# mLSTM steps put ahead of attention's in the emission order, and side work on TensorE emitted only where its operands are modelled as ready some time ahead

## The chip, the cores and the metric

The kernel runs on one core of one Trainium2 chip. A core has TensorE (PE) for matmuls, VectorE (DVE), ScalarE (ACT) and GpSimd (POOL) for elementwise work, and SyncE (SP), whose queue issues the transfers. Each engine takes its own instructions in order; semaphores hold an instruction back until what it reads has been written. The metric is the device time of one execution in microseconds, as the median of several runs. Before the change it was 1105.98 us over three runs (1102.45 to 1107.39).

## The reference

One layer of a decoder, for a prompt of 512 positions and a group of 8 samples of one position each, which share all weights (D_MODEL 1024, all in float32):

```python
z = rmsnorm(h) @ w_in                       # q, k, v of attention; q, k, v, o, gates of the mLSTM; two gates
o_a = attention of three dilation groups, 12 heads of 64, merged by softmax of their log sums
      # prompt: banded blocks of 128;  sample: 129 gathered positions of the caches per head
qk = silu(causal_conv(z[..., OFF_MQ:OFF_MV], conv_buf, conv_w, conv_b))
hm, C1, n1, m1 = mlstm(qm, km, vm, ig, lf, C0, n0, m0)   # 4 heads of 256, chunked scan over the prompt,
                                                         # one step for each sample with its state C0
o_b = rmsnorm_per_head(hm) * mh_norm * sigmoid(z_o)
mix = sigmoid(g_a) * (o_a @ w_proj_a) + sigmoid(g_b) * (o_b @ w_proj_b)
h = h + mix @ w_out
h = h + (silu(xf @ w_gate) * (xf @ w_up)) @ w_down       # xf = rmsnorm(h)
h = h + sigmoid(xp @ w_ple_gate) * (p @ w_ple_proj)      # xp = rmsnorm(h)
```

It returns the normed outputs, the updated key and value caches, the convolution rows, and the mLSTM states C, n and m of the prompt and of the samples.

## The kernel before

**Dense work.** The weights stream through in chunks of 512 rows. Each is split in two float32r parts, whi (a cast on ScalarE or VectorE) and wlo (the rest, on VectorE), and so is the activation (xnh and xnl, or "pieces"). A product is three matmuls, hi by hi, hi by lo and lo by hi, on halves of 260 columns (512 + 8 positions make 520). The products with w_pb and with the gate and up weights of the feed-forward part go by seven combined products instead of eight, which need sums of weights (ws) and sums of activations (ta, tb, piece). The order of all dense jobs is one list, `order`; `dense_to` (line 672) walks through it.

**Side work.** Everything else is written as Python generators that `yield` a condition and then emit an instruction: attention of the prompt (`attn_prompt`), of the samples (`attn_sample`), the mLSTM of the prompt (`mlstm_prompt`) and of the samples (`sample_rows`, `sample_loads`, `mlstm_sample` with its two `steps`, `sample_sums`), the evictions and norms. Between the matmuls of a dense product `dense_to` calls `feed`, which loads and splits weights ahead, and `pr.run()` of the class `Procs` (line 305), which goes through all waiting generators, evictions (`evs`) first, then `live` in the order in which they were spawned, and lets each go on as far as its condition holds.

**What sets the order.** While it emits, the program keeps a model of the five engines, `Clock`: for each a time at which it is free, and for each tile the time at which it is written and read. The condition `on(engs, *tiles, **rooms)` (line 271) asks whether the rings of the named tags have room and whether the tiles are ready in the model: for TensorE at the model's present time, for others within a limit. If no dense product can go on, `stall` moves the model's TensorE 0.1 on. The settings in `PAR` are by stage: A to the end of the products with w_in that attention and the mLSTM need (variable `n_win`), then B, C and D.

**Rings.** Tiles come from rings by tag. S has five slots: attention's loaded cache rows (kvb, in triples, one for each dilation group), the state tiles ct of the mLSTM and others share it. P1 and P2 hold the broadcast rows qb and kb of the samples' mLSTM, and later the tanh tiles of the gates (th), which are to be written only when the last `sample_loads` is done. PSUM has two pairs of banks for dense results (pp) and four banks b for the rest.

**Names in the rows.** All instructions are issued through one helper, so each row carries its line, L225. pT is the transposed softmax of sample attention, `pT,kvb` its product with loaded value rows; qkm the samples' q and k rows; yc the convolved rows, whose last step also leaves nout; numv and dns the numerators and denominators of the samples' mLSTM; W0 to W3 the prompt's mLSTM weights; scs the scores of sample attention; raw a loaded weight.

Of the kernel before, what the change touches and what calls it, by code (L numbers as in the profile page):

```python
# [32 lines left out]
def kernel(tc, a):  # L33
# [8 lines left out]


PAR = {
    "A": dict(LIM=1.8, SLACK=1.5, THIN=0.8, BIAS=0.3, EVLIM=2.0, PLIM=0.3),
    "B": dict(LIM=0.8, SLACK=0.51, THIN=0.8, BIAS=0.24, EVLIM=1.97, PLIM=0.01),
    "C": dict(LIM=1.59, SLACK=0.52, THIN=0.8, BIAS=0.02, EVLIM=2.16, PLIM=0.5),
    "D": dict(LIM=1.28, SLACK=1.14, THIN=0.8, BIAS=0.32, EVLIM=1.71, PLIM=0.38),
}


# [178 lines left out]
def _body(nc, a, const, sb, psp, drp):  # L230
# [10 lines left out]
    def tl(tag, name, shape=None, dt=F32):  # L241
        w = WIDTH.get(tag, 520)
        if tag in used:
            used[tag] += 1
        return ck.new(sb.tile(list(shape or (128, w)), dt, name=name, tag=tag, bufs=NB[tag]), tag, NB[tag])
# [8 lines left out]
    def bank(shape=(128, 512)):  # L254
        used["b1"] += 1
        return ck.new(psp.tile(list(shape), F32, name="b1", tag="b1", bufs=4), "b1", 4)
# [7 lines left out]
    def free(n, tag):  # L264
        used[tag] -= n
# [3 lines left out]
    P = dict(PAR["A"])  # L269

    def on(engs, *tiles, lim=None, **rooms):

        engs = engs.split()

        def ok():
            for tag, n in rooms.items():
                if tag in used and used[tag] + n > NB[tag]:
                    return False
            now = ck.t["pe"]
            for tag, n in rooms.items():  # L280
                i = ck.count.get(tag, 0)
                if any(ck.idle(tag, i + j, NB[tag]) > now + P["SLACK"] for j in range(n)):
                    return False
            if engs[0] == "pe":
                t = now
            else:
                t = min(ck.t[e] for e in engs)
                if t > now + (P["LIM"] if lim is None else lim):
                    return False
                t = max(t, now) + 0.1  # L290
            return all(ck.ready(x) <= t for x in tiles)
        return ok

    class Cycle:
        def __init__(self, tags):
            self.tags, self.i = tags, 0

        def next(self, n):
            return [self.tags[(self.i + k) % len(self.tags)] for k in range(n)]
# [4 lines left out]

    class Procs:
        def __init__(self):
            self.evs, self.live = [], []

        def spawn(self, gen, first=False):
            (self.evs if first else self.live).append([None, gen])  # L310

        def run(self):
            for q in (self.evs, self.live):
                for p in list(q):
                    while p[0] is None or p[0]():
                        try:
                            p[0] = next(p[1])
                        except StopIteration:
                            q.remove(p)
                            break  # L320

    pr = Procs()
# [35 lines left out]
    def copy(dst, src, names=("act", "dve")):  # L358
        n = pick(names, "tensor_copy", dst, [src])
        if n == "act":  # L360
            S_.copy(dst, src)
        else:
            ENG[n].tensor_copy(dst, src)
# [5 lines left out]
    def stt(dst, x, sc, y, op0, op1):  # L369
        V.scalar_tensor_tensor(dst, x, sc, y, op0=op0, op1=op1)  # L370
# [956 lines left out]
    def sample_rows(h):  # L1327

        yield lambda: all(("k", h, dt) in ml for dt in range(2)) and "rows" in flag
        yield on("pe", qkm, b1=1, S=1)  # L1330
        bk = bank((8, 2, 2, 128))
        rows = tl("S", "mrows", (8, 2, 256))
        for w in range(2):
            for dt in range(2):
                PE.transpose(bk[:, w, dt], qkm[:, h, w, dt], ident)
        yield on("act dve", bk)
        copy(rows.rearrange("b w d -> b (w d)"), bk.rearrange("b w t d -> b (w t d)"))
        free(1, "b1")
        yield on("sp", rows)
        dr = drp.tile([8, 2, 256], F32, name="mdr", tag="mdr", bufs=2)  # L1340
        SP.dma_start(dr.rearrange("b w d -> b (w d)"), rows.rearrange("b w d -> b (w d)"))
        free(1, "S")
        mdr[h] = dr
# [18 lines left out]
    def mlstm_sample(h):  # L1362
        yield lambda: (h, 0) in cts and all(("v", h, vt) in ml for vt in range(2))
        yield on("dve", vm, s24b)
        vw = sb.tile([128, 2, 8], F32, name="vw", tag="vw", bufs=2)
        V.tensor_tensor(vw, vm[:, h], s24b[:, h, 8:16].unsqueeze(1).to_broadcast([128, 2, 8]), op=ALU.mult)
        numv = sb.tile([128, 2, 8], F32, name="numv", tag="numv", bufs=2)
        left = [8]

        def steps(b0):  # L1370
            for b in range(b0, 8, 2):
                yield lambda: (h, b) in cts
                cur = cts.pop((h, b))
                qb, kb = qks[h, b - b % 2]
                yield on("act dve", cur, s24b)
                if pick(("act", "dve"), "tensor_scalar", cur, [cur]) == "act":
                    S_.activation(cur, cur, AF.Copy, scale=s24b[:, h, b:b + 1])
                else:
                    V.tensor_scalar(cur, cur, s24b[:, h, b:b + 1], None, op0=ALU.mult)
                for vt in range(2):  # L1380
                    yield on("dve", cur, kb, vw)
                    stt(cur[:, vt], kb[:, b % 2], vw[:, vt, b:b + 1], cur[:, vt], ALU.mult, ALU.add)
                for vt in range(2):
                    yield on("dve", cur, qb)
                    V.tensor_tensor_reduce(junk, cur[:, vt], qb[:, b % 2], 1.0, 0.0, ALU.mult, ALU.add,
                                           numv[:, vt, b:b + 1])
                left[0] -= 1
                done[b] = True
                if b ^ 1 in done:
                    free(1, "P1")  # L1390
                    free(1, "P2")
                store(a["C_s"][h, b], cur, lambda: free(1, "S"))

        done = {}
        for b0 in range(2):
            pr.spawn(steps(b0))
        yield lambda: left[0] == 0
        pr.spawn(sample_sums(h, numv))

    def sample_sums(h, numv):  # L1400

        nn = nout[:, h, :, 1:9]
        w_i = s24b[:, h, 8:16].unsqueeze(1).to_broadcast([128, 2, 8])
        w_x = s24b[:, h, 0:8].unsqueeze(1).to_broadcast([128, 2, 8])
        nt = small(32, "nt").rearrange("p (t c) -> p t c", t=2)
        tv = nt[:, :, 0:8]
        V.tensor_tensor(tv, qkm[:, h, 1], w_i, op=ALU.mult)
        V.tensor_tensor(nn, nst[:, h], w_x, op=ALU.mult)
        V.tensor_tensor(nn, nn, tv, op=ALU.add)
        V.tensor_tensor(tv, nn, qkm[:, h, 0], op=ALU.mult)  # L1410
        V.tensor_tensor(nt[:, :, 8:16], numv, numv, op=ALU.mult)
        yield on("pe", nt, b1=1)
        bk = bank((128, 16))
        for t in range(2):
            PE.matmul(bk, ones, nt[:, t], start=t == 0, stop=t == 1)

        dn = sb.tile([128, 16], F32, name="dns", tag="dns", bufs=2)
        yield on("act", bk)
        S_.activation(dn[:, 0:8], bk[:, 0:8], AF.Abs)
        V.tensor_copy(dn[:, 8:16], bk[:, 8:16])  # L1420
        free(1, "b1")
        yield on("dve", dn)
        V.tensor_tensor(dn[:, 0:8], dn[:, 0:8], s24b[:, h, 16:24], op=ALU.max)
        ml["ns", h] = True
        yield lambda: ("og", h, 0) in ml and ("og", h, 1) in ml
        yield from sample_out(h, numv, dn)
# [163 lines left out]
    def chain(*gens):  # L1590
        for g in gens:
            yield from g
# [113 lines left out]
    def loads():  # L1706
        for c in "0a123":
            if c == "a":
                yield lambda: "vs" in flag
            else:  # L1710
                yield from sample_loads(int(c))
# [4 lines left out]
    for c in "apm":  # L1716
        if c == "a":
            pr.spawn(chain(attn_prompt(0), attn_prompt(1)))
        elif c == "p":
            pr.spawn(chain(*[mlstm_prompt(h) for h in range(4)]))  # L1720
        else:
            pr.spawn(samples())
            pr.spawn(loads())
            pr.spawn(chain(*[sample_rows(h) for h in range(4)]))
            pr.spawn(chain(*[mlstm_sample(h) for h in range(4)]))

    oa = []

# [393 lines left out]
    for h in range(2):  # L2122
        pr.spawn(last_norm(h))
    dense_to(len(order))
    while pr.evs or pr.live:
        stall()
    while copies:
        cache_copy()
# [141 lines left out]
```

## Time and profile before

| | us |
|---|---|
| median of 3 runs (lowest to highest) | 1105.98 (1102.45 to 1107.39) |
| profiled execution | 1104.25 |
| its span in the trace | 1102.5 |
| TensorE busy | 1050.2 (95%) |
| VectorE busy | 859.1 (78%) |
| ScalarE busy | 522.8 (47%) |
| GpSimd busy | 35.8 (3%) |
| mean granted clock of TensorE | 0.979 of full |

The span is the time between the first and the last instruction in the trace; the rest of the profiled execution, 1.75 us, lies around it. Idle time of an engine is shown with what ended it. The granted clock is the share of full speed that TensorE was given: 1.00 is 2.4 GHz and 0.50 is 1.2 GHz. A time in the text is counted from the start of the span. "Dense columns" count the columns of the dense matmuls emitted so far; they give a place in the program that is the same in both kernels, since the list of dense jobs isn't changed.

### The profile page before, as it was taken

Reading aid. Unit: us, or ns where it says so; the run is one execution under the profiler, and the core shown is the slowest. Engines: PE = TensorE matmul, PEld = TensorE weight load, DVE = VectorE, ACT = ScalarE, POOL = GpSimd, SP = SyncE. Lnnn points to the kernel's source line nnn. Section 1 sums busy time; section 2 is a strip of 40 time slices with the busy share of each in tenths; the row PEclk is TensorE's granted clock in tenths of the full one; section 3 lists DMA queues with packets and bytes.
Section 4 is the critical chain, followed back from the end, with each engine's and each line's share of the span. In section 5 each row is a group of like instructions: output and inputs, shape, how many; then the busy total and the mean of one; then the engine's idle time right before and its main releaser. Section 6 shows DMA issues by size and latency. Waiting matters only on the chain.

```text
span 1102.5 us, 21771 instructions
## 1 busy us (share of the span) xinstructions
PE 1050.2 (95%) x8404; PEld 1026.4 (93%) x8404; DVE 859.1 (78%) x1768; ACT 522.8 (47%) x968; POOL 35.8 (3%) x126
## 2 busy tenths in 40 slices
PE   7999999999998999997999999989999999999995
PEld 6999899999998989996999999989999999999995
DVE  7994559877778599876466868999888888866775
ACT  6445444664454487754343335435344434433553
POOL 0010010001001011000000000000000000000000
PEclk9999999999997999998999999999999999999998
DMA  6365157747846986876566833322323332333321
GB/s 229 118 201 174 58 193 244 269 150 227 269 138 218 309 268 197 268 213 227 197 210 233 283 103 96 121 84 92 103 83 108 111 101 83 110 94 97 120 83 59
DMA packets 90904, 180.21 MB, mean 163 GB/s; under 512 B 11604, under 2 KB 37252, under 8 KB 89392
## 3 DMA queue, kind: packets, MB, share of 16 engines
q1 hardware_dynamic: 90800, 178.82, 50.5%
q8 instruction: 66, 1.08, 0.4%
q14 instruction: 38, 0.31, 0.1%
HBM read 163.65 MB, written 59.13 MB: 202 GB/s over the span
## 4 chain that ended last, share of the span: by engine, by line
PE 67%; DVE 15%; DMA 8%; ACT 5%; issue 3%; SPq 1%; POOL 0%; DVEq 0%; ACTq 0%
PE pp L225 42%; PE b L225 25%; DVE wlo L225 3%; DMA raw<-in_w_in 3%; DVE yc L225 2%; ACT whi L225 2%; DMA out_C_s<-ct 1%; DMA ct<-in_sC 1%; DMA qb<-mdr 1%; DVE ct L225 1%; SPq L225 1%; DVE junk L225 1%; DVE piece L225 1%; DVE sw L225 1%; DVE h L225 1%
## 5 line engine op out<-in xcount | busy, mean ns | idle before, releaser
L225 DVE TENSOR_TENSOR wlo<-raw,whi 128x512 fp32r<-128x512 f32 (+3 forms) x358 | 236.6, 664 | 148.1 <-ACT whi L225 134.5
L225 ACT CAST whi<-raw 128x512 fp32r<-128x512 f32 (+3 forms) x340 | 203.1, 601 | 290.8 <-PE pp L225 155.3
L225 PE MATMUL b<-piece,whi 128*128 128x260 f32 x1232 | 229.3, 287 | 10.0 <-ACT piece L225 6.0
L225 PE MATMUL pp<-xnh,whi 128*128 128x260 f32 x1008 | 209.4, 289 | 0.8 <-ACT th L225 0.8
L225 PE MATMUL pp<-xnh,wlo 128*128 128x260 f32 x1008 | 208.4, 288 | 0.0
L225 PEld LDWEIGHTS b<-piece,whi 128*128 128x128 f32 x1232 | 194.5, 193 | 12.1 <-ACT piece L225 6.7
L225 PE MATMUL pp<-xnl,whi 128*128 128x260 f32 x1008 | 204.8, 285 | 0.8 <-DVE xnl L225 0.7
L225 PE MATMUL b<-piece,wlo 128*128 128x260 f32 x616 | 176.7, 287 | 0.1
L225 PEld LDWEIGHTS pp<-xnh,whi 128*128 128x128 f32 x1008 | 157.4, 191 | 2.2 <-ACT th L225 1.0
L225 PEld LDWEIGHTS pp<-xnl,whi 128*128 128x128 f32 x1008 | 157.9, 191 | 1.2 <-DVE xnl L225 1.2
L225 PEld LDWEIGHTS pp<-xnh,wlo 128*128 128x128 f32 x1008 | 157.4, 191 | 1.1
L225 PEld LDWEIGHTS b<-piece,wlo 128*128 128x128 f32 x616 | 118.6, 193 | 0.6 <-DVE wlo L225 0.6
L225 PE MATMUL pp<-hpl,whi 128*128 128x260 f32 x352 | 70.8, 282 | 0.0
L225 PE MATMUL pp<-hph,whi 128*128 128x260 f32 x352 | 70.8, 282 | 0.0
L225 PE MATMUL pp<-hph,wlo 128*128 128x260 f32 x352 | 70.7, 282 | 0.0
L225 PEld LDWEIGHTS pp<-hpl,whi 128*128 128x128 f32 x352 | 54.2, 188 | 0.0
L225 PEld LDWEIGHTS pp<-hph,wlo 128*128 128x128 f32 x352 | 54.2, 188 | 0.0
L225 PEld LDWEIGHTS pp<-hph,whi 128*128 128x128 f32 x352 | 54.2, 188 | 0.0
L225 ACT CAST whi<-ws 128x512 fp32r<-128x512 f32 x29 | 17.9, 621 | 57.1 <-PE b L225 48.5
L225 DVE TENSOR_TENSOR uv<-uv,b 128x260 f32<-128x260 f32 (+1 forms) x88 | 42.7, 485 | 0.0
L225 DVE SCALAR_TENSOR_TENSOR yc<-zc,par,yc 128x552 f32<-128x552 f32 x48 | 37.8, 788 | 5.0 <-ACT yc L225 4.5
L225 PE MATMUL pp<-mix,whi 128*128 128x260 f32 x256 | 41.1, 282 | 0.0
(383 smaller groups left out, 1875.3 us busy)
## 6 DMA issues: line engine op xcount, KB each, us to landing
raw<-in_w_in SPq DMA_DIRECT2D x132, 256.0 KB, 3.5
out_kvout<-in_cache SPq DMA_DIRECT2D x64, 512.0 KB, 4.6
raw<-in_w_gate SPq DMA_DIRECT2D x44, 256.0 KB, 3.6
raw<-in_w_up SPq DMA_DIRECT2D x44, 256.0 KB, 4.4
ct<-in_sC SPq DMA_DIRECT2D x32, 256.0 KB, 6.6
out_C_s<-ct SPq DMA_DIRECT2D x32, 256.0 KB, 4.4
raw<-in_w_down SPq DMA_DIRECT2D x32, 256.0 KB, 2.6
out_kvout<-in_cache SPq DMA_DIRECT2D x16, 510.0 KB, 4.9
```

What stands on the lines that cost most here:

```text
L225: fn(*args, **kw)
```

## The change

The settings get a new entry, SURE: 0.4 in stage A and 0.0 in the others. `on` subtracts it from the time at which a step on TensorE must find its operands ready. `Procs` gets a third list, `urgent`, which `run` goes through after `evs` and ahead of `live`. The prompt's mLSTM, the loads of the samples' mLSTM and its other generators are spawned into it; attention of the prompt and of the samples stays in `live`.

```diff
@@ -42,10 +42,10 @@
 
 
 PAR = {
-    "A": dict(LIM=1.8, SLACK=1.5, THIN=0.8, BIAS=0.3, EVLIM=2.0, PLIM=0.3),
-    "B": dict(LIM=0.8, SLACK=0.51, THIN=0.8, BIAS=0.24, EVLIM=1.97, PLIM=0.01),
-    "C": dict(LIM=1.59, SLACK=0.52, THIN=0.8, BIAS=0.02, EVLIM=2.16, PLIM=0.5),
-    "D": dict(LIM=1.28, SLACK=1.14, THIN=0.8, BIAS=0.32, EVLIM=1.71, PLIM=0.38),
+    "A": dict(SURE=0.4, LIM=1.8, SLACK=1.5, THIN=0.8, BIAS=0.3, EVLIM=2.0, PLIM=0.3),
+    "B": dict(SURE=0.0, LIM=0.8, SLACK=0.51, THIN=0.8, BIAS=0.24, EVLIM=1.97, PLIM=0.01),
+    "C": dict(SURE=0.0, LIM=1.59, SLACK=0.52, THIN=0.8, BIAS=0.02, EVLIM=2.16, PLIM=0.5),
+    "D": dict(SURE=0.0, LIM=1.28, SLACK=1.14, THIN=0.8, BIAS=0.32, EVLIM=1.71, PLIM=0.38),
 }
 
 
@@ -282,7 +282,7 @@
                 if any(ck.idle(tag, i + j, NB[tag]) > now + P["SLACK"] for j in range(n)):
                     return False
             if engs[0] == "pe":
-                t = now
+                t = now - P["SURE"]
             else:
                 t = min(ck.t[e] for e in engs)
                 if t > now + (P["LIM"] if lim is None else lim):
@@ -304,13 +304,13 @@
 
     class Procs:
         def __init__(self):
-            self.evs, self.live = [], []
-
-        def spawn(self, gen, first=False):
-            (self.evs if first else self.live).append([None, gen])
+            self.evs, self.urgent, self.live = [], [], []
+
+        def spawn(self, gen, first=False, urgent=False):
+            (self.evs if first else self.urgent if urgent else self.live).append([None, gen])
 
         def run(self):
-            for q in (self.evs, self.live):
+            for q in (self.evs, self.urgent, self.live):
                 for p in list(q):
                     while p[0] is None or p[0]():
                         try:
@@ -1393,9 +1393,9 @@
 
         done = {}
         for b0 in range(2):
-            pr.spawn(steps(b0))
+            pr.spawn(steps(b0), urgent=True)
         yield lambda: left[0] == 0
-        pr.spawn(sample_sums(h, numv))
+        pr.spawn(sample_sums(h, numv), urgent=True)
 
     def sample_sums(h, numv):
 
@@ -1717,12 +1717,12 @@
         if c == "a":
             pr.spawn(chain(attn_prompt(0), attn_prompt(1)))
         elif c == "p":
-            pr.spawn(chain(*[mlstm_prompt(h) for h in range(4)]))
+            pr.spawn(chain(*[mlstm_prompt(h) for h in range(4)]), urgent=True)
         else:
             pr.spawn(samples())
-            pr.spawn(loads())
-            pr.spawn(chain(*[sample_rows(h) for h in range(4)]))
-            pr.spawn(chain(*[mlstm_sample(h) for h in range(4)]))
+            pr.spawn(loads(), urgent=True)
+            pr.spawn(chain(*[sample_rows(h) for h in range(4)]), urgent=True)
+            pr.spawn(chain(*[mlstm_sample(h) for h in range(4)]), urgent=True)
 
     oa = []
 
@@ -2122,7 +2122,7 @@
     for h in range(2):
         pr.spawn(last_norm(h))
     dense_to(len(order))
-    while pr.evs or pr.live:
+    while pr.evs or pr.urgent or pr.live:
         stall()
     while copies:
         cache_copy()
```


What this does to the order of the instructions is shown at three places.

VectorE, at the start of the products with w_pb, before: numv, th and dns close the last head of the samples' mLSTM, ta, tb and piece make its activations, ws sums weights.

```order
L225 SCALAR_TENSOR_TENSOR th<-th,pp 128x520
L225 SCALAR_TENSOR_TENSOR dns<-dns 128x8
L225 RECIPROCAL dns<-dns 128x8
L225 TENSOR_TENSOR numv<-numv,dns 128x16
L225 SCALAR_TENSOR_TENSOR th<-th,numv 128x8 x2
L225 TENSOR_TENSOR ta<-th 128x260
L225 TENSOR_TENSOR piece<-th,piece 128x260
L225 TENSOR_TENSOR ta<-th 128x260
L225 TENSOR_TENSOR piece<-th,piece 128x520
L225 TENSOR_TENSOR ws<-raw 128x512
L225 TENSOR_TENSOR ws<-ws,raw 128x512
L225 TENSOR_TENSOR tb<-ta,th 128x260
```

The same place after the change:

```order
L225 RECIPROCAL dns<-dns 128x8
L225 TENSOR_TENSOR numv<-numv,dns 128x16
L225 SCALAR_TENSOR_TENSOR th<-th,numv 128x8 x2
L225 TENSOR_TENSOR ta<-th 128x260
L225 TENSOR_TENSOR piece<-th,piece 128x260
L225 TENSOR_TENSOR ta<-th 128x260
L225 TENSOR_TENSOR piece<-th,piece 128x520
L225 TENSOR_TENSOR tb<-ta,th 128x260
L225 TENSOR_TENSOR wlo<-raw,whi 128x256
L225 TENSOR_TENSOR tb<-th,tb 128x260
L225 CAST piece<-ta 128x520
L225 TENSOR_TENSOR piece<-ta,piece 128x520
```

The reciprocal and the steps ta, tb and piece have moved ahead of the weight sums and of the gate steps (`th<-th,pp`), and splits of weights for the products before w_pb now stand among them.

SyncE's queue, the loads of the last two triples of cached values (kvb) for sample attention, before:

```order
L225 DMA kvb<-in_cache 128x2x256 x3
L225 DMA raw<-in_w_in 128x512
L225 DMA wkb<-drow 128x512
L225 DMA kvb<-in_cache 128x2x256 x3
L225 DMA raw<-in_w_in 128x512
L225 DMA out_kvout<-in_cache 16x8192
L225 DMA raw<-in_w_in 128x512
L225 DMA kvb<-in_cache 128x2x256 x3
```

And after:

```order
L225 DMA out_C_p<-cp 128x256
L225 DMA raw<-in_w_in 128x512
L225 DMA kvb<-in_cache 128x2x256 x3
L225 DMA raw<-in_w_in 128x512
L225 DMA out_kvout<-in_cache 16x8192
L225 DMA kvb<-in_cache 128x2x256 x3
L225 DMA raw<-in_w_in 128x512
L225 DMA kvb<-in_cache 128x2x256 x3
```

The last triple is issued one weight load behind the one before it; before, two weight loads and a cache copy stood between them, and wkb, a broadcast row, is now issued later.

TensorE, the end of the value part, before: the products of the last triple are b_4403.

```order
L225 MATMUL pp<-xnh,wlo 128x260 x2
L225 MATMUL pp<-xnh,whi 128x260 x2
L225 MATMUL pp<-xnl,whi 128x260 x2
L225 MATMUL b_4403<-pT,kvb 128x2 x3
L225 MATMUL pp<-xnh,wlo 128x260 x2
L225 MATMUL b_4403<-pT,kvb 128x2 x3
L225 MATMUL pp<-xnh,whi 128x260 x2
L225 MATMUL pp<-xnl,whi 128x260 x2
L225 MATMUL b_4403<-pT,kvb 128x2 x3
L225 MATMUL pp<-xnh,wlo 128x260 x2
```

After the change they are b_4204.

```order
L225 MATMUL b_4119<-pT,kvb 128x2 x3
L225 MATMUL pp<-xnh,whi 128x260 x2
L225 MATMUL pp<-xnl,whi 128x260 x2
L225 MATMUL pp<-xnh,wlo 128x260 x2
L225 MATMUL pp<-xnh,whi 128x260 x2
L225 MATMUL pp<-xnl,whi 128x260 x2
L225 MATMUL pp<-xnh,wlo 128x260 x2
L225 MATMUL pp<-xnh,whi 128x260 x2
L225 MATMUL pp<-xnl,whi 128x260 x2
L225 MATMUL b_4204<-pT,kvb 128x2 x12
L225 MATMUL pp<-xnh,wlo 128x260 x2
```

The dense matmuls between the triples have become fewer, and the groups of the last triple now stand in one piece.

## Rows read from the trace of the kernel before

**Rows 1.** The page: busy time of each engine, busy tenths and clock in 40 slices.

```profile
PE 1050.2 (95%) x8404; PEld 1026.4 (93%) x8404; DVE 859.1 (78%) x1768; ACT 522.8 (47%) x968; POOL 35.8 (3%) x126
...
PE   7999999999998999997999999989999999999995
...
PEclk9999999999997999998999999999999999999998
```

**Rows 2.** Stretches: us, busy us (instructions) of each engine, granted clock, DMA.

```profile
70.00:339.00 269.00, 259.67 (x2072) 250.06 (x2070) 199.20 (x475) 138.20 (x286) 20.83 (x83) 0.99 0.61 195
252.00:320.00 68.00, 64.48 (x513) 62.70 (x513) 54.02 (x115) 31.98 (x60) 6.08 (x26) 0.97 0.70 220
339.00:360.00 21.00, 16.96 (x94) 16.45 (x95) 15.81 (x42) 9.10 (x15) 2.60 (x8) 0.67 0.59 202
360.00:495.00 135.00, 130.47 (x1031) 126.51 (x1031) 112.03 (x289) 88.36 (x161) 9.14 (x27) 1.00 0.78 254
495.00:527.00 32.00, 23.94 (x156) 21.79 (x155) 18.97 (x51) 13.53 (x25) 0.00 (x0) 0.84 0.61 200
```

**Rows 3.** Waits of TensorE: for what, us in total, times, longest.

```profile
PE pp L225 <- ACT th L225: 2.6, 3, 1.0
...
PE b L225 <- DVE W3l L225: 1.3, 2, 0.9
```

**Rows 4.** Timeline of TensorE at the first w_pb products: start, us, work [idle before].

```profile
514.31 0.85 PE L225 MATMUL b<-piece,whi 128*128 128x260 f32 x2 [2.81 <-ACT piece L225]
...
517.71 0.80 PE L225 MATMUL b<-piece,whi 128*128 128x260 f32 x2 [0.53 <-ACT whi L225]
...
522.17 0.58 PE L225 MATMUL b<-piece,whi 128*128 128x260 f32 x1 [1.85 <-ACT piece L225]
522.90 0.59 PE L225 MATMUL b<-piece,whi 128*128 128x260 f32 x1 [0.15 <-DVE piece L225]
```

**Rows 5.** Stretches at the lower clock, columns as in rows 2.

```profile
341.00:349.00 8.00, 8.00 (x43) 7.97 (x44) 5.19 (x11) 3.60 (x6) 1.49 (x3) 0.57 0.83 310
352.00:359.00 7.00, 5.46 (x27) 5.47 (x27) 6.70 (x24) 2.80 (x6) 0.00 (x0) 0.51 0.48 147
516.00:526.00 10.00, 7.46 (x30) 6.34 (x30) 7.42 (x14) 3.53 (x6) 0.00 (x0) 0.50 0.31 105
```

**Rows 6.** Timeline of VectorE at the first w_pb products.

```profile
511.96 0.20 DVE L225 RECIPROCAL dns<-dns 128x8 f32<-128x8 f32 x1 [0.71 <-ACT dns L225]
...
515.59 0.69 DVE L225 TENSOR_TENSOR ws<-raw 128x512 f32<-128x512 f32 x1
```

**Rows 7.** Timeline of TensorE, value part of sample attention and what follows.

```profile
325.32 0.72 PE L225 MATMUL b<-pT,kvb 128*128 128x2 f32 x6
...
329.35 0.72 PE L225 MATMUL b<-pT,kvb 128*128 128x2 f32 x6
...
332.32 0.72 PE L225 MATMUL b<-pT,kvb 128*128 128x2 f32 x6
...
337.77 0.50 PE L225 MATMUL b<-pT,kvb 128*128 128x2 f32 x4
339.91 0.38 PE L225 MATMUL b<-pT,kvb 128*128 128x2 f32 x2 [1.63 <-DMA kvb<-in_cache]
...
351.03 0.27 PE L225 MATMUL b<-cstA,qkm 128*8 128x128 f32 x1 [1.59 <-POOL qkm L225]
...
353.56 1.08 PE L225 MATMUL b<-cstA,yc 128*128 128x128 f32 x4 [1.54 <-DVE nout L225]
```

**Rows 8.** Instructions of the tile kvb: its loads, and their landing times.

```profile
L225 SPq DMA_DIRECT2D kvb<-in_cache x24: 367/432/1059, 234.9 to 334.7; - x24
...
DMA to landing us min/median/max: 3.5/4.3/4.9
```

**Rows 9.** Timeline of SyncE's queue: the loads of the last triple.

```profile
333.08 2.08 SPq L225 DMA_DIRECT2D kvb<-in_cache  x3
```

## Prediction

> **What bounds the kernel now.** I read the totals of the page first: TensorE is busy 1050.2 of 1102.5 us at a full granted clock in nearly every slice, with dips in slice 13 (331 to 358 us), slice 19 (496 to 524 us) and the last [rows 1]. VectorE is next at 859.1 us, ScalarE has half of that. The change adds and removes no matmul: both orders hold 8220 of them with 2,087,574 columns. So it can only win back TensorE's idle time and its time at the lower clock, or add to them. The table of stretches shows where these are [rows 2]: from 70 to 339 us TensorE is idle 269.00 - 259.67 = 9.3 us, from 339 to 360 us 4.0, from 360 to 495 us 4.5, from 495 to 527 us 8.1 of 32 us. In the second and the fourth the clock is low too, 0.67 and 0.84 on average. Then I read who is waited for [rows 3] and, at the two bad places, the single gaps [rows 4, 7].
>
> PE's order is the same in both kernels up to about 70 us and from about 510 us on, so what lies outside (the start, the waits of the later products, the end) stays; I count nothing for it.
>
> **Part one: the start of the w_pb products, 498 to 526 us.** TensorE waits 2.6 us in three pieces for gate tiles (th) [rows 3], then 2.81 us for the first piece of the last head, 0.53 us for a weight, 1.85 + 0.15 us for later pieces [rows 4]: 8.0 us. From 516 to 526 us the clock is at its lower level, 0.50 of full, which is 1.2 GHz [rows 5]. TensorE is busy 7.46 us there, of which half, 3.7 us, is the price of the clock. Together 11.7 us.
>
> The cause is the last link of the sample's mLSTM. The reciprocal of its denominators runs on VectorE at 511.96 us, all that makes the last head's pieces stands behind it, and the weight sums ws behind those pieces (515.59) [rows 6]. In the changed order VectorE's steps for the pieces stand ahead of ws and of the th steps (first order fences). The loads of the last sample rows (qb, kb, ct) come 47 to 52 thousand dense columns earlier, and the reciprocal and the pieces 16 to 20 thousand columns before w_pb's first product instead of behind it. At 2400 columns a microsecond (0.127 us a matmul from 360 to 495 us [rows 2], most of them of 260 columns) that is a lead of 7 to 8 us against waits of at most 2.81 us: these go. The th tiles share the rings P1 and P2 with qb and kb; with those loads done early each is emitted at the end of its own job and no longer behind the last load, so the 2.6 us go too. What is late next is the weights: the wait of 0.53 us is for whi and not for a piece, so I keep it, and 0.5 us for a wait that I can't see. Value: -11.7 + 1.0 = -10.7 us. Bounds: -11.7, and -5.3 if the weights' own sums, cast and split (two ws of 0.69 us each [rows 6], and a cast and a split of about the same) become a wait of 2.7 us and the dip of 3.7 us stays.
>
> **Part two: 339 to 360 us.** TensorE waits 1.63 us for a sample's value rows (kvb), 1.59 us for qkm and 1.54 us for yc, put down to nout [rows 7]: 4.76 us. The clock is low twice, 8.00 x (1 - 0.57) = 3.4 us and 5.46 x (1 - 0.51) = 2.7 us [rows 5]. Together 10.9 us. The demand that operands be ready 0.4 us ahead moves qkm and yc: the matmul work between the producer and the transposes grows from about 0.2 to 1.4 us and from 1.4 to 3.1 us (columns of the order at 2400 a microsecond), by about as much as the waits. These two go.
>
> The kvb wait doesn't. The value part of sample attention works through four triples of loads in a ring of five slots, so the third load of a triple waits for the last product with the triple before. For the last triple the issues begin at 333.08 us and last 2.08, and TensorE, which is at its first group at 337.77, stands until 339.91 [rows 7, 9]: 6.9 us behind the last group of the previous triple, which ended at 333.0 (332.32 + 0.72). The third triple had 3.3 us (326.04 to 329.35; 325.32 + 0.72) and no wait. Between the triples stood 24, 28 and 40 dense matmuls; now it is 20 products of the mLSTM and 6 dense matmuls, 16 dense and two of 512 columns, and 16 dense (third order fences): covers of 3.3, 2.3 and 2.0 us. With 3.3 us from last product to landing the new waits are 0 + 1.0 + 1.3 = 2.3 us, with 6.8 us 3.5 + 4.5 + 4.8 = 12.8 us. I take the median landing of 4.3 us and 0.4 us for its issue [rows 8], 1.4 + 2.4 + 2.7 = 6.5 us. After such a wait and the thin products around it the clock fell once, at 341 to 349 us; I count one such dip, 3.4 us, with bounds of 0 and 6.1 us (both). Part two: -10.9 + 6.5 + 3.4 = -1.0 us, from -8.6 to +8.0.
>
> The Trainium skill ("DMA: Bandwidth & Descriptors", section "Anatomy of one DMA — SWDGE (gpsimd) path") puts a transfer at about 2.0 us fixed plus its bytes at 436 GB/s, on another issuing path; for 256 KB that is an estimate of 2.6 us. By it the three waits would be 0, 0.3 and 0.6 us, and the sum 5.6 us lower; the trace's landing of 3.5 to 4.9 us [rows 8] disagrees.
>
> **Part three: the rest.** W3l stands twice as far behind its producers as before and loses its 0.9 us [rows 3]. Of the other 8 us of idle time between 70 and 339 us some waits gain lead (yc, scs) and some lose it: the product with cstB near 131 us has 0.7 us of matmul work ahead of it instead of 2.4. I hold these at nothing, with 3 us on either side. Seven steps that go to ScalarE instead of VectorE are hidden: ScalarE is idle a third of even its busiest stretch, 360 to 495 us [rows 2].
>
> **Sum.** -10.7 - 1.0 - 0.9 = -12.6 us. The profiled execution took 1104.25 us (span 1102.5 and 1.75 around it), 1.73 us under the median of 1105.98. So 1091.7 us for such an execution and 1093 us as a median. Here a time is told from no change at about 0.5%, 5.5 us: faster is under 1100.5, slower over 1111.5.
>
> **Rivals.**
> *More is won.* The rows land in 3.3 us and no dip follows: part two is -8.6 and part one -11.7, with part three -21.2 us, 1084.8 us; with its 3 us 1082. For it: the third triple before. Against it: the last triple, and a cover of 2.0 us under the shortest landing, 3.5 us. 0.17.
>
> *The value rows eat it.* All three triples land as the last did and both dips are paid: part two is +8.0, the sum -10.7 + 8.0 - 0.9 = -3.6, the time 1102.4; no change that can be told. For it: the one wait for kvb came with twice the cover. Against it: its loads were issued 1.7 us late, at 334.7 and not at 333.0. 0.19.
>
> *The weights are late at w_pb*, and the change doesn't do what it seems to there: -5.3 - 1.0 - 0.9 = -7.2, the time 1098.8. For it: ws needs VectorE, ScalarE and VectorE again in a row. Against it: in the changed order it stands ahead of w_pb and of nothing late. 0.10.
>
> *VectorE becomes the bound, slower than before.* Between 370 and 460 thousand dense columns (252 to 320 us) VectorE gets 136 instructions instead of 116; at 54.02 us for 115 [rows 2] that is 64 us of work in a stretch of about 73, 88%. It takes its queue in order, so a weight split behind the mLSTM steps, which now go first, comes late, TensorE idles and its clock falls. What such a time costs shows from 339 to 360 us [rows 2]: 4.0 us idle and 16.96 x 0.33 = 5.6 us of clock, 9.6 of 21 us or 46%. All of the 73 us would cost 33.6 us; with the 10.7, 10.9 and 0.9 us taken off, 1105.98 - 22.5 + 33.6 = 1117. It is slower from 28.0 us lost on, 61 us of that stretch. For it: 88% is more than in any stretch of the table. Against it: from 360 to 495 us VectorE is busy 83% and TensorE loses 4.5 of 135 us. 0.08.
>
> **Chances and range.** My forecast, 1093 us with 1087 to 1099 of its own, has 0.46. Faster: 0.46 + 0.17, 0.08 of the late weights and 0.02 of the eaten case, 0.73. Same: the other 0.02 and 0.17, 0.19. Slower: 0.08. The range for 8 in 10 goes from 1081, the larger gain with a little over its 3 us, to 1105; beyond lie the slower case and the worst of the eaten one.
>
> **What would show it.** Right: the last head's reciprocal well ahead of the first w_pb products, no piece wait and no half clock there, no th waits; none for qkm and yc near 350 us; three gaps of 1 to 3 us for kvb, now at about 310 to 325 us, and one dip behind them. Wrong: gaps for wlo or whi between 250 and 330 us (the VectorE case), pieces still waited for at w_pb, or kvb without a gap (the larger gain).

## The result and the profile after

| | before | after |
|---|---|---|
| median, us | 1104.78 (6 runs, 1102.45 to 1107.39) | 1097.97 (6 runs, 1095.95 to 1100.86) |
| ratio, 95% interval | | 0.9941 (0.9918 to 0.9963) |
| profiled execution, us | 1104.25 | 1100.63 |
| its span, us | 1102.5 | 1098.8 |

The change makes the kernel 6.8 us faster. The forecast was 1093 us, 12.6 us faster: the direction holds, the gain is about half of it. A profile shows one execution, which can lie some us from the median: the change's took 1100.63 us, 2.7 over its median, and its second one ("The change once more") 1102.65, 4.8 over (those of the experiments lie up to 6.9 us off), so the losses read in them are larger than a median execution's, and no profile shows how the 6.8 us are made up.

The page of the changed kernel, busy time and granted clock in 40 slices, to be read against [rows 1]:

```profile
PE 1049.3 (95%) x8404; PEld 1026.6 (93%) x8404; DVE 854.2 (78%) x1761; ACT 522.4 (48%) x975; POOL 42.3 (4%) x126
...
PEclk9999999998988999999999999999999999999998
```

TensorE's total hardly moves. The dip of slice 19 is gone, and there are now dips in slice 10 (247 to 275 us) and in slices 12 and 13 (302 to 357 us).

Stretches of the changed kernel, columns as in [rows 2] and [rows 5]:

```profile
323.00:337.00 14.00, 14.00 (x69) 14.00 (x69) 9.34 (x18) 4.25 (x6) 1.19 (x3) 0.52 0.69 218
337.00:372.00 35.00, 31.43 (x256) 30.27 (x256) 32.22 (x81) 17.84 (x33) 8.44 (x20) 1.00 0.82 270
396.00:416.00 20.00, 17.66 (x129) 16.47 (x129) 19.90 (x50) 12.58 (x23) 6.80 (x14) 1.00 0.73 225
395.00:423.00 28.00, 23.59 (x175) 21.98 (x174) 24.99 (x60) 16.97 (x32) 6.80 (x14) 0.99 0.79 260
423.00:495.00 72.00, 69.20 (x537) 67.11 (x537) 64.27 (x169) 51.88 (x95) 3.48 (x5) 0.98 0.71 231
495.00:527.00 32.00, 31.86 (x267) 31.65 (x266) 26.49 (x63) 17.64 (x32) 0.00 (x0) 1.00 0.69 243
```

From 495 to 527 us TensorE is busy 31.86 of 32 us at full clock, where it lost 8.1 us and part of the clock before. In return, from 323 to 337 us it is busy all the time at about half the clock, and from 395 to 423 us it is idle 4.4 of 28 us. VectorE is busy 24.99 us there, and without a pause from 396 to 416 us (19.90 of 20).

TensorE's timeline after (start, us, work, [idle before]), the value part, some waits, and the first product with w_pb:

```profile
320.13 0.38 PE L225 MATMUL b<-pT,kvb 128*128 128x2 f32 x2 [0.20 <-DMA kvb<-in_cache]
320.79 0.38 PE L225 MATMUL b<-pT,kvb 128*128 128x2 f32 x2 [0.28 <-DMA kvb<-in_cache]
...
323.42 1.13 PE L225 MATMUL b<-pT,kvb 128*128 128x2 f32 x6
324.41 0.78 PE L225 MATMUL pp<-xnh,whi 128*128 128x260 f32 x2
...
328.02 5.17 PE L225 MATMUL b<-pT,kvb 128*128 128x2 f32 x24
333.06 0.78 PE L225 MATMUL pp<-xnh,wlo 128*128 128x260 f32 x2
...
357.71 0.51 PE L225 MATMUL pp<-xnh,wlo 128*128 128x260 f32 x2 [1.68 <-DVE wlo L225]
...
361.81 0.66 PE L225 MATMUL b<-cstA,yc 128*128 128x128 f32 x4 [0.46 <-DVE nout L225]
...
367.80 0.27 PE L225 MATMUL b<-cstA,qkm 128*8 128x128 f32 x1 [0.46 <-POOL qkm L225]
...
408.58 0.33 PE L225 MATMUL b<-W3h,vmh 128*128 128x128 f32 x1 [0.68 <-ACT W3h L225]
410.35 0.33 PE L225 MATMUL b<-W3l,vmh 128*128 128x128 f32 x1 [1.45 <-DVE W3l L225]
...
421.36 0.66 PE L225 MATMUL b<-cstA,yc 128*128 128x128 f32 x4 [2.06 <-DVE nout L225]
...
515.11 0.40 PE L225 MATMUL b<-piece,whi 128*128 128x260 f32 x2
```

That first product stood here in the kernel before:

```profile
510.28 0.40 PE L225 MATMUL b<-piece,whi 128*128 128x260 f32 x2
```

So TensorE comes to w_pb 4.8 us *later* than before (515.11 against 510.28), and its net gain comes from there on. VectorE after, near the W3l wait, and at w_pb, against [rows 6]:

```profile
408.11 0.68 DVE L225 TENSOR_TENSOR wlo<-raw,whi 128x512 fp32r<-128x512 f32 x1
408.71 0.69 DVE L225 SCALAR_TENSOR_TENSOR mql<-yc,mqh 128x512 fp32r<-128x512 f32 x1
409.31 0.79 DVE L225 SCALAR_TENSOR_TENSOR yc<-zc,par,yc 128x552 f32<-128x552 f32 x1
410.01 0.28 DVE L225 TENSOR_TENSOR W3l<-Wf,W3h 128x128 fp32r<-128x128 f32 x1
...
504.72 0.20 DVE L225 RECIPROCAL dns<-dns 128x8 f32<-128x8 f32 x1
...
510.43 0.69 DVE L225 TENSOR_TENSOR piece<-tb,piece 128x520 fp32r<-128x520 f32 x1
...
511.37 0.68 DVE L225 TENSOR_TENSOR ws<-raw 128x512 f32<-128x512 f32 x1
```

The reciprocal runs 10.4 us ahead of w_pb and the last piece is done at 511.1 us, 4 us ahead; before, both came behind w_pb's start.

The two traces can be laid over each other by counting the dense matmuls of 260 columns, which come in the same order. For each stretch of dense columns (thousands): TensorE's idle time, and half of its busy time at the lower clock, in us, before and after. The last column is the same change read from the change's second profile:

| columns | idle | low clock | sum of the two, change | second profile |
|---|---|---|---|---|
| 0 to 52 | 7.5, 7.7 | 0, 1.7 | +2.0 | +0.4 |
| 52 to 416 | 7.2, 6.7 | 3.4, 5.1 | +1.1 | +3.7 |
| 416 to 520 (value part, qkm, yc) | 7.6, 5.9 | 6.1, 6.8 | -1.0 | -0.3 |
| 520 to 728 (heads 2 and 3 of the mLSTM) | 4.7, 7.9 | 0, 1.7 | +5.0 | +5.5 |
| 728 to 780 (first w_pb products) | 7.3, 0.0 | 3.9, 0.0 | -11.2 | -11.2 |
| 780 to the last matmul | 8.6, 12.3 | 3.5, 1.7 | +1.9 | +2.0 |

By elapsed time the fifth row is 36.97 us before and 23.95 after, 13.0 us less. The 1.8 us that the table doesn't hold are busy time: the pair of matmuls behind the first wait is in work for 0.85 us (514.31 [rows 4]) where a pair took 0.40 (510.28), and four small matmuls of the mLSTM stand in that stretch only before. TensorE's order is the same in both kernels in the first row and, but for one swap near 1060 us, in the last; VectorE's differs in both, from 27 us on.

### The profile page after: what moved, and what is told of

Its sections match the earlier page's. It is cut to its first block, busy times and chain, and to the rows that moved or that the text cites. A ratio compares the mean times of both kernels' runs of the same rounds, so it can differ in the third digit from the quotient of the medians.

```text
span 1098.8 us, 21784 instructions
## 1 busy us (share of the span) xinstructions
PE 1049.3 (95%) x8404; PEld 1026.6 (93%) x8404; DVE 854.2 (78%) x1761; ACT 522.4 (48%) x975; POOL 42.3 (4%) x126
## 4 chain that ended last, share of the span: by engine, by line
PE 77%; DVE 11%; DMA 7%; issue 2%; ACT 2%; SPq 1%; DVEq 0%; POOL 0%; ACTq 0%
PE pp L225 49%; PE b L225 28%; DMA ct<-in_sC 3%; DVE wlo L225 2%; DVE yc L225 1%; DMA raw<-in_w_in 1%; SPq L225 1%; DVE ct L225 1%; DMA raw<-in_w_pg 1%; ACT whi L225 1%; DVE junk L225 1%; DVE h L225 0%; DMA rC<-in_rope 0%; DMA xr<-in_xT 0%; DMA kvb<-in_cache 0%
## 5 line engine op out<-in xcount | busy, mean ns | idle before, releaser
L225 PE MATMUL b<-piece,whi 128*128 128x260 f32 x1232 | 223.9, 283 | 4.4 <-DVE piece L225 1.5
L225 PEld LDWEIGHTS b<-piece,whi 128*128 128x128 f32 x1232 | 190.9, 189 | 5.2 <-issue 1.9
L225 PE MATMUL pp<-x3h,whi 128*128 128x260 f32 x128 | 37.1, 290 | 3.5 <-DVE gs L225 3.5
```

What stands on the lines that cost most here:

```text
L225: fn(*args, **kw)
```

## The experiments

Each is the changed kernel with the edit that is shown, timed in five rounds beside the kernel before. Ratios are to the kernel before.

**The demand alone.**

```diff
-pr.spawn(chain(*[mlstm_prompt(h) for h in range(4)]), urgent=True)
+pr.spawn(chain(*[mlstm_prompt(h) for h in range(4)]))
...   (and every other urgent=True taken out)
```

> The demand for 0.4 us alone, no urgent list. The last head's reciprocal comes 19 thousand columns before w_pb in the order (723.8 against 742.6). Theory (the gain of 13 us at w_pb needs only that this chain ends 7 us ahead): the gaps at w_pb are gone and the time is 1094 to 1100 us. Rival (the urgent list is what brings the gain at w_pb): the piece and th waits stay for the most part, 1102 us or more.

Measured: 1108.93 us, ratio 1.0024 (1.0004 to 1.0044); no gain. TensorE's timeline ahead of w_pb:

```profile
500.03 0.80 PE L225 MATMUL pp<-xnh,whi 128*128 128x260 f32 x2 [12.74 <-ACT th L225]
```

The pieces are early, as expected (728 to 780 thousand columns take 13.0 us less), but the wait has only moved: it stands on a gate tile, 12.74 us, since the loads of the last sample rows come as late as before and hold the rings P1 and P2: the last qb is issued at 711 thousand columns, before at 710, in the change at 655. (Why that costs 12.74 us here and 2.6 before isn't shown.) The theory that the chain's place alone decides is wrong, and the rival has the right number for another reason.

**The urgent list alone.**

```diff
-    "A": dict(SURE=0.4,
+    "A": dict(SURE=0.0,
```

> The urgent list alone, the demand set to 0 in all stages. In the order it is the kernel before up to 530 thousand columns, and the reciprocal of the last head comes 41 thousand before w_pb. Theory (part one by itself): 13 us less at w_pb, the waits and the low clock at 339 to 360 us as before, and no loss between 520 and 728 thousand columns, because that comes from the demand for 0.4 us: 1091 to 1094 us. Rival (the loss there comes from the mLSTM steps run first): 1097 to 1100 us, with 5 us or more lost in that stretch.

Measured: 1093.09 us, ratio 0.9886 (0.9857 to 0.9914), 4.9 us faster than the change. Three stretches of it:

```profile
313.00:321.00 8.00, 8.00 (x38) 7.67 (x36) 1.24 (x2) 1.80 (x4) 0.00 (x0) 0.57 0.46 155
344.00:362.00 18.00, 14.51 (x75) 13.90 (x74) 13.83 (x38) 7.20 (x12) 1.68 (x4) 0.62 0.60 213
480.00:527.00 47.00, 46.70 (x391) 46.49 (x390) 38.54 (x85) 25.89 (x45) 0.00 (x0) 1.00 0.70 230
```

The 13.0 us at w_pb are there (480 to 527 us hardly idle, full clock), and the low clock at 344 to 362 us stays. The one at 313 to 321 us has no counterpart in the profile of before, though TensorE's order is the same in both up to 370 us and its one wait ahead of it too (0.99 us for scs): it is this execution's. Between 520 and 728 thousand columns TensorE idles 4.4 us, as before (4.7) and not 7.9. Part one is worth what it was put at, without the demand; in this order the demand costs 5 us on top.

**Only the samples' mLSTM urgent**, no demand.

```diff
-    "A": dict(SURE=0.4,
+    "A": dict(SURE=0.0,
...
-pr.spawn(chain(*[mlstm_prompt(h) for h in range(4)]), urgent=True)
+pr.spawn(chain(*[mlstm_prompt(h) for h in range(4)]))
```

> Only the samples' mLSTM (its rows, loads, steps and sums) goes into the urgent list, the prompt's mLSTM stays behind attention; no demand for lead. The last reciprocal stands 50 thousand columns before w_pb, but the prompt's last head comes later (its norm sums at 726 thousand instead of 663). Theory (what has to be early at w_pb is the samples' chain): the 13 us at w_pb are won, 1091 to 1095 us. Rival (the pieces need the prompt's rows as well, so these become what is waited for): piece waits of 2 us or more at w_pb and 1098 us or more.

Measured: 1109.72 us, ratio 1.0033 (1.001 to 1.0056). The rival holds:

```profile
519.77 1.05 PE L225 MATMUL b<-piece,whi 128*128 128x260 f32 x2 [6.16 <-DVE piece L225]
```

**Only the prompt's mLSTM urgent**, no demand.

```diff
-    "A": dict(SURE=0.4,
+    "A": dict(SURE=0.0,
...
-pr.spawn(loads(), urgent=True)
+pr.spawn(loads())
...   (and so for sample_rows, mlstm_sample, steps and sample_sums)
```

> Only the prompt's mLSTM goes into the urgent list, no demand for lead. The last reciprocal stands 8 thousand columns, 3.5 us, ahead of w_pb instead of behind its start. Theory (the samples' chain and its loads set the waits at w_pb): less than half of the 13 us is won, 1100 to 1105 us, with a gate tile waited for while the loads are late. Rival (a lead of 3.5 us is over every wait there, so it is enough): 1092 to 1096 us.

Measured: 1100.57 us, ratio 0.9956 (0.9931 to 0.9981), as the theory said: 4.7 of the 13.0 us are won at w_pb, and gate tiles and a piece are still waited for.

```profile
497.00 0.51 PE L225 MATMUL pp<-xnh,whi 128*128 128x260 f32 x2 [2.27 <-ACT th L225]
...
507.69 0.51 PE L225 MATMUL pp<-oah,whi 128*128 128x260 f32 x2 [2.21 <-DVE th L225]
...
515.73 0.38 PE L225 MATMUL b<-piece,whi 128*128 128x260 f32 x1 [2.40 <-ACT piece L225]
```

**All but the step processes urgent.**

```diff
-            pr.spawn(steps(b0), urgent=True)
+            pr.spawn(steps(b0))
```

> The changed kernel with only the two step processes of the samples' mLSTM (scaling, update and sums of the state tiles, the VectorE work) put back into the late list. Theory (their place on VectorE decides when the rings come free): the last loads come late again, a gate tile is waited for as with the demand alone, for 5 us or more, and the time is 1101 to 1109 us. Rival (these steps crowd VectorE ahead of the weights W of the prompt's mLSTM, and without them in front the waits for W3l and nout go): 1094 us or less.

Measured: 1109.68 us, ratio 1.0041 (1.0018 to 1.0063). It is the theory's case, a little above its bound. The gate tile's wait is back, and the last qb is again issued at 711 thousand columns, as the theory has it (the steps on VectorE free the rings that the loads need):

```profile
506.37 0.80 PE L225 MATMUL pp<-xnh,whi 128*128 128x260 f32 x2 [12.40 <-ACT th L225]
```

Together the five say that of the parts tried only the prompt's and the samples' mLSTM in front, steps included, win the whole 13 us: with the demand alone, or with the steps left behind, they are won at w_pb and lost to a gate tile just ahead of it.

**More room between thin products, 2.0 us.**

```diff
-    "A": dict(SURE=0.4, LIM=1.8, SLACK=1.5, THIN=0.8,
+    "A": dict(SURE=0.4, LIM=1.8, SLACK=1.5, THIN=2.0,
```

> The changed kernel with the distance between groups of thin value products raised from 0.8 to 2.0 us in stage A, so that they lie spread over 438 to 496 thousand columns. Theory (the thin products crowded into 438 to 455 thousand columns hold the clock low for 13.7 us): no such stretch, no more than 3.5 us of low clock there, and 5 us less in it, 1093 us unless the later chain costs it again. Rival (the clock fell through something else there): the low stretch stays over 10 us, 1097 to 1099 us.

Measured: 1097.42 us, ratio 0.9927 (0.9901 to 0.9953). The low stretch is gone: between 416 and 520 thousand columns no time is lost to the clock, against 6.8 us. But sample attention now ends late, the last qb is issued at 711 thousand columns, and gate tiles are waited for; this is the case that the theory left open with "unless the later chain costs it again":

```profile
490.04 0.80 PE L225 MATMUL pp<-xnh,whi 128*128 128x260 f32 x2 [6.79 <-ACT th L225]
...
500.08 0.51 PE L225 MATMUL pp<-xnh,whi 128*128 128x260 f32 x2 [2.33 <-ACT th L225]
```

**The same, 1.0 us.**

```diff
-    "A": dict(SURE=0.4, LIM=1.8, SLACK=1.5, THIN=0.8,
+    "A": dict(SURE=0.4, LIM=1.8, SLACK=1.5, THIN=1.0,
```

> The changed kernel with 1.0 instead of 0.8 us between groups of thin value products: the last triple's four groups, 24 thin matmuls in one piece before, are spread over 461 to 466 thousand columns, and the later chain hardly moves (last reciprocal at 720 instead of 718 thousand). Theory (the crowded thin products hold the clock low): the low stretch near 323 to 337 us shrinks from 13.7 us to 7 or less, 3 us or more are won there, 1092 to 1095 us. Rival (it is low for another reason): 10 us or more of low clock there, 1097 to 1100 us.

Measured: 1083.71 us, ratio 0.9804 (0.9768 to 0.984): the fastest kernel of this study, 14 us faster than the change, and outside both forecasts. Four groups of its last triple, and two stretches:

```profile
329.43 0.72 PE L225 MATMUL b<-pT,kvb 128*128 128x2 f32 x6
...
330.82 0.73 PE L225 MATMUL b<-pT,kvb 128*128 128x2 f32 x6
...
332.22 0.72 PE L225 MATMUL b<-pT,kvb 128*128 128x2 f32 x6
...
333.61 0.72 PE L225 MATMUL b<-pT,kvb 128*128 128x2 f32 x6
```

```profile
323.00:337.00 14.00, 14.00 (x121) 14.00 (x121) 12.02 (x21) 7.78 (x11) 2.69 (x8) 1.00 0.86 281
390.00:415.00 25.00, 25.00 (x199) 24.46 (x198) 24.69 (x58) 16.78 (x30) 5.82 (x16) 1.00 0.83 253
```

The groups stand 1.39 us apart with dense matmuls between, and from 323 to 337 us the clock is full, where the change has 0.52: the theory of the clock holds, and more is won there than the 3 us expected (no low clock from 416 to 468 thousand columns, 6.8 us in the change). Beyond that, idle time and low clock between 572 and 676 thousand columns fall from 8.7 us to 0.5: head 2 of the prompt's mLSTM stands 13 thousand columns earlier in this order, and none of its W tiles is waited for long. That was not expected. As for the clock, the other kernels say the same: all ten kernels of this study with 0.8 us between groups have a stretch of low clock among the value products or right behind them (the change in both its profiles), and the three with 1.0, 1.2 and 2.0 us have none there.

**Sample attention urgent too.**

```diff
-            pr.spawn(samples())
+            pr.spawn(samples(), urgent=True)
```

> The changed kernel with sample attention put into the urgent list too, ahead of the samples' mLSTM. The value products lie at 449 to 468 thousand columns, the groups still in order. Theory (crowding of the value products decides the clock there): they are a little less crowded, low clock of 7 to 14 us, 1095 to 1099 us. Rival (attention's place behind the mLSTM's steps costs): 1092 us or less.

Measured: 1087.01 us, ratio 0.983 (0.9802 to 0.9859). The clock at its value part and at yc, where nout is waited for 3.7 us:

```profile
326.00:337.00 11.00, 11.00 (x70) 11.00 (x70) 7.14 (x17) 4.42 (x6) 0.43 (x3) 0.69 0.87 272
353.00:361.00 8.00, 6.46 (x33) 6.46 (x34) 7.36 (x17) 3.76 (x9) 1.30 (x3) 0.57 0.65 216
```

Between 326 and 361 us the clock falls in three pieces of 3.4 to 6.8 us instead of one of 13.7; 572 to 676 thousand columns idle 2.0 us instead of 7.0. Both theories have a share in it: the time is the rival's, the clock's part the theory's.

**The same without the demand.**

```diff
-    "A": dict(SURE=0.4,
+    "A": dict(SURE=0.0,
...
-            pr.spawn(samples())
+            pr.spawn(samples(), urgent=True)
```

> Sample attention in the urgent list as in attn_urgent, but without the demand for 0.4 us of lead. Theory (the demand pays where sample attention isn't starved, by the waits for qkm, yc and the like): 4 to 7 us slower than attn_urgent, 1091 to 1094 us. Rival (the demand costs here as it costs in the change, 5 us): 1081 to 1084 us.

Measured: 1095.96 us, ratio 0.9908 (0.9873 to 0.9944), 8.9 us slower than with it. Here the demand pays, as the theory has it and by more, where in the change it costs. Without it there are two long low stretches, one at the value part and one at qkm and yc:

```profile
318.00:332.00 14.00, 14.00 (x67) 13.81 (x66) 8.71 (x16) 4.36 (x6) 0.51 (x4) 0.52 0.47 150
341.00:356.00 15.00, 12.76 (x63) 12.46 (x63) 7.40 (x23) 2.91 (x5) 1.11 (x3) 0.54 0.81 263
```

**The same with a demand of 0.3 us.**

```diff
-    "A": dict(SURE=0.4,
+    "A": dict(SURE=0.3,
...
-            pr.spawn(samples())
+            pr.spawn(samples(), urgent=True)
```

> attn_urgent with a demand of 0.3 instead of 0.4 us. The second head of the prompt's mLSTM stands 15 thousand columns earlier (its norm sums at 555 instead of 577 thousand, and the first part at 541 instead of 555), the last reciprocal at 718 as in the change. Theory (the loss after 520 thousand columns comes from head 2 standing late, close to the samples' steps on VectorE): no W3l wait over 0.5 us, 1084 to 1089 us. Rival (0.4 us is what pays by the waits for qkm, yc and cstB): 1091 us or more.

Measured: 1100.34 us, ratio 0.9957 (0.9934 to 0.998). The W3l wait is gone, as the theory has it (0.23 us), but the time is the rival's. Of the rival's waits the one for cstB's operand t has grown (2.4 us against 0.5 with 0.4 us), the one for nout has not (3.1 against 3.7), so neither side explains the 13 us between the two kernels:

```profile
PE b L225 <- DVE nout L225: 3.1, 2, 2.9
PE b L225 <- DVE t L225: 2.4, 1, 2.4
PE b L225 <- ACT W2h L225: 2.3, 2, 2.0
```

This profile also shows the clock fall without any wait ahead of it. From 305.5 us on TensorE has no idle time and works through four groups of thin value products, the last two of them in one row from 309.27 us; during these, at 310.2 us, the clock falls:

```profile
305.50:310.20 4.70, 4.70 (x43) 4.70 (x42) 3.49 (x12) 2.73 (x6) 0.08 (x1) 1.00 0.00 0
310.20:313.70 3.50, 3.50 (x14) 3.21 (x14) 2.65 (x7) 1.04 (x2) 0.38 (x3) 0.51 0.64 186
```

**Sample attention urgent, 1.2 us between thin products.**

```diff
-    "A": dict(SURE=0.4, LIM=1.8, SLACK=1.5, THIN=0.8,
+    "A": dict(SURE=0.4, LIM=1.8, SLACK=1.5, THIN=1.2,
...
-            pr.spawn(samples())
+            pr.spawn(samples(), urgent=True)
```

> attn_urgent with 1.2 us instead of 0.8 between groups of thin value products, which then lie at 449 to 486 thousand columns. Theory (crowded thin products hold the clock low): less low clock between 320 and 365 us than attn_urgent's 13.7 us, by half or more, and 1082 to 1086 us if the later chain of the sample's second head (reciprocal at 597 instead of 524 thousand columns) costs nothing. Rival (later loads make gate tiles or pieces wait, as with 2.0 us): 1088 us or more.

Measured: 1088.32 us, ratio 0.9837 (0.9805 to 0.9869). No time at the low clock is left between 416 and 520 thousand columns, but 7.9 us of it are lost between 624 and 728 thousand, and a gate tile is waited for 4.4 us, the rival's case; the two cancel.

```profile
PE pp L225 <- ACT th L225: 4.4, 1, 4.4
```

**The change once more**, for a second profile.

> The changed kernel as it is, beside the next three on one chip, and a second profile of it. If the dip of the clock at 20 us and the wait of 2.2 us near 1051 us in its first profile are chance, they are gone or elsewhere in this one; the low stretch at 323 to 337 us and the waits for W3l (410 us) and nout (421 us) come from the order and are there again. 1096 to 1100 us.

Measured: 1097.86 us, ratio 0.9929 (0.9907 to 0.9952). The low stretch and the W3l wait are there again, the dip at 20 us and the wait of 2.2 us near 1051 us aren't, nor is the longer nout wait of 421 us.

```profile
324.00:339.00 15.00, 14.55 (x74) 14.46 (x74) 9.74 (x18) 4.52 (x6) 1.18 (x3) 0.54 0.68 204
```

```profile
412.18 0.33 PE L225 MATMUL b<-W3l,vmh 128*128 128x128 f32 x1 [1.45 <-DVE W3l L225]
```

## Why the prediction was right in direction and high in size

*Part one*, forecast -10.7 us: right in its cause, and a little small. The waits for pieces and gate tiles and the low clock at w_pb are gone, 13.0 us by elapsed time, 1.3 over its larger bound. What was expected to be late next, a weight, isn't waited for; the 1.0 us held back for it was not needed, and the longer work behind waits had no term. The lead was put at 7 to 8 us with 2400 columns a microsecond, which doesn't follow from 0.127 us a matmul (260 columns in that are about 2050); it came out at 10.4 us. The chain of causes holds in the experiments: the waits follow the last sample rows and pieces (urgent list), and the th waits follow the loads' hold on P1 and P2: in the six kernels that issue the last qb at 689 thousand columns or later TensorE waits 2.6 us or more for gate tiles (12.74 in the kernel with the demand alone), and in the seven that issue it at 655 to 678 not at all, but for 0.96 us in the kernel with only the samples' mLSTM in front.

*Part two*, forecast -1.0 us: the sum comes out, -1.0 by idle time and clock (-0.3 in the second profile), but by luck: two of its terms are wrong and cancel. The waits for kvb were put at 6.5 us and are 0.5 (0.20 at 320.13 and 0.28 at 320.79). From the last product with a triple (ended 317.3) to the last data of the third triple (320.79) it took 3.5 us, not 4.7; in the 4.7 the issue's 0.4 us stands twice, since the landing of 4.3 us is counted from the start of the issue. The data of the last triple was there when TensorE came, since the clock had fallen and the 16 dense matmuls ahead of it took 3.6 us (324.41 to 328.02) instead of 2.0.

The clock was put at one dip of 3.4 us and costs 6.8. It falls at 323.6 us, in the last group of the third triple (323.42, 1.13 us instead of 0.72), and stays low through the 24 thin matmuls in one row (328.02, 5.17 us) to 337.2 us, without any idle time. That the crowding brings this is shown by the kernel with 1.0 us between the groups: the same products, spread, at full clock, with one wait of 0.30 us for kvb still among them. The change's fall does stand behind its two short waits, but it needs none: the kernel with a demand of 0.3 us falls without one (310.2 us). A wait can do it as well, as the prediction had it: the kernel with 1.0 us falls for 3.4 us at 354.5 us, behind a wait of 2.47 us for z.

The qkm and yc waits fell from 3.1 to 1.3 us (0.46, 0.46, 0.41 at 361.81, 367.80 and 370.88) and didn't go entirely, and a new wait for a weight's low part took 1.68 us of it (357.71), which no term had.

*Part three* is the step that failed: -0.9 us, 3 us either way, where the runs show +1.1 up to 416 thousand columns and +5.0 between 520 and 728 (+3.7 and +5.5 in the second profile). Of the latter only W3l had a term at all. I had W3l lose its wait because "W3l stands twice as far behind its producers as before". That distance I had read from W0, the first of the four tiles. By the order, the first product with W0l stands 8.4 us of columns behind the scores that W0 is made from before, and 16.4 after; for W3l it is 4.1 and 5.2, and its wait grew from 0.9 [rows 3] to 1.45 us, with 0.68 us for W3h ahead of it. In both places the queue of VectorE stands between: from 396 to 416 us it has no idle time, and W3l (410.01), whose input W3h was done at 408.53, runs behind mql and a convolution step; before, it ran 1.3 us behind W3h (394.60 against 393.26). Nothing that I had counted showed that, because a distance in TensorE's columns says nothing of how far VectorE is behind. It is not fullness alone either: the kernel with 1.0 us between groups has VectorE busy 24.69 of 25 us from 390 to 415 us and a distance of 4.7 us for W3l, and TensorE is idle for none of it: W3l (394.95) is done 0.5 us ahead of its first product. So what makes TensorE wait is the step's place in VectorE's queue against TensorE's, and that no count of columns gives. Most of the rest of the +5.0 is one wait of 2.06 us for nout (421.36) with a fall of the clock right behind it; the second profile has that fall behind W3l instead, and not this wait.

*The rest.* 0 to 52 thousand columns and the end were counted at nothing. The first profile has 2.0 and 1.9 us more there, mostly the low clock at 20 us and one wait of 2.2 us for gs, neither of which the second profile has, so these belong to one execution. But the second has 2.0 us more at the end as well, there by the clock; whether the change costs something at the end stays open.

*The rivals.* VectorE as the bound was placed at 252 to 320 us and came, in small, at 395 to 423 us: 4.4 us idle and one fall of the clock for 3.4 us behind it (422.6 us), far from the 28 us it needed. The value rows did not eat the gain by waiting; their crowding ate 6.8 us by the clock. The larger gain had the waits nearly right, 0.5 us where it put 2.3, but it wanted no dip behind them, and there is one of 13.6 us. The weights were not late.

What stays open: why the plan with a demand of 0.3 us is 13 us slower than that with 0.4. Each setting gives another order for the whole of stage A, and the waits of 1 to 3 us fall in other places; no single cause was isolated for that.

## What to carry to other kernels

An edit to a planner's rules has one effect that can be priced from the trace (the wait that the rules were changed for) and many that can't, since all that follows is ordered anew; here these took back half of a gain that was sized right, and a setting changed by 0.2 us gave 14 us more. So price the aimed wait, and give the reshuffled rest a cost of its own with a wide range, not zero. And look at where an edit bunches thin matmuls: here they showed as a fully busy TensorE, without a wait, and still cost half of their stretch.

## What the runs showed of the hardware

TensorE busy without a gap can still be at the lower clock: from 323 to 337 us of the changed kernel busy 14.00 of 14 us at a mean granted clock of 0.52, during and around 24 matmuls of two columns in a row; in groups of six, spread 1.39 us apart, the same products ran at 1.00. And the clock differs between executions of one program: the dip at 20 us is in the first profile of the change and not in the second, and in five of the fourteen profiles in all. It differs behind the same wait, too: behind 0.99 us for scs near 310 us the kernel with the urgent list alone fell to the low clock at 313.4 us, and the kernel before, with the same matmuls, stayed at full clock.
